# Layer 0's input product in two halves of its contraction, in a two-layer attention encoder

## The chip, the cores and the metric

The kernel runs on one core of one Trainium2 chip. The metric is device time of one execution in microseconds (us), and less is better. The engines are TensorE (PE in the profile; its weight loads are PEld), VectorE (DVE), ScalarE (ACT), GpSimd (POOL) and SyncE (SP), whose queue issues nearly all DMA transfers, in program order.

## The reference

One sequence of 256 tokens, width 2048, passes two layers. Each layer makes six modulation vectors from a conditioning vector, projects the normed and modulated stream by one wide matrix, runs two kinds of attention on the pieces, joins them in an output projection, and adds an MLP. The inputs and all weights are float32.

```python
cond = jax.nn.silu(c)
for l in range(DEPTH):
    mod = cond @ w_ada[l] + b_ada[l]                  # 2048 -> 6 * 2048
    sh_a, sc_a, g_a, sh_m, sc_m, g_m = split(mod, 6)
    h = _rmsnorm(x) * (1.0 + sc_a) + sh_a
    proj = h @ w_in[l]                                # 2048 -> 3904
    # dq 1024 | dk 1024 | dv 1024 | cq 512 | ckv 256 | kr 64
    out_a = _diff_attention(dq, dk, dv, positions, rel_bias_table, lam, subln_g, lambda_init)
    q  = _rmsnorm(cq, q_norm_g[l]) @ w_uq[l]          # 8 heads, 128 + 64 rotated
    kv = _rmsnorm(ckv, kv_norm_g[l]) @ w_ukv[l]       # 8 heads, 128 keys + 128 values
    out_b = _mla_attention(q_nope, q_rope, k_nope, k_rope, v_m)
    x = x + g_a * (concat([out_a, out_b]) @ w_o[l])
    h = _rmsnorm(x) * (1.0 + sc_m) + sh_m
    x = x + g_m * (square(relu(h @ w_mlp_in[l])) @ w_mlp_out[l])   # 2048 -> 8192 -> 2048
return _rmsnorm(x, final_norm_g)
```

The differential attention has 4 heads of two score maps each, with a bias that is looked up by bucketed distance between tokens. The multi-head latent attention (MLA below) has 8 heads with rotated parts.

## The kernel before

**Layout.** Features lie on the 128 partitions and tokens along the free axis, so x and h are 16 pieces of 128 x 256, one for each k (128 rows of the contraction). A tile of an output is 128 features by 256 tokens; two tiles share one of the eight PSUM banks (512 floats per partition).

**Two ways to multiply.** *Split*: `weights()` (L137) loads up to 1 MB into a buffer of the tag `raw`, ScalarE copies each half to a rounded `hi` (L146), VectorE subtracts to get `lo` (L147), and a tile takes three matmuls for each k (hi x hi, hi x lo, lo x hi; L182 to L184 in `mac()`, L253 to L255 for values, whose tokens lie on partitions). *Native*: the float32 weights are loaded straight into buffers of the tags `hi` and `lo` (L228) and multiplied without any split (L239); a matmul of this kind shows two records in the trace. Tags `hi` and `lo` have 4 buffers each, `raw` has 5.

**Modulation.** `ada_load()` (L289) brings one 128 x 2048 block (1 MB) of `w_ada` into a `raw` buffer, and `ada_sums()` (L297) multiplies it by the conditioning row `cond` on VectorE and sums along the row, which makes one column of one modulation vector. There are 192 such blocks in all. Every second sum is followed by a small operation that adds the constant part for two columns (L311 or L313). `ada_need()` brings all blocks up to one that is about to be used. Beside that each call of `weights()` adds a rate (`self.rate`) to a credit, and a block is loaded for each whole credit; the rate is `RATE_A0` = 1.1 in layer 0's attention. Layer 0's first 32 blocks, shift and scale, are needed by the input product.

**The head of layer 0.** `setup()` (L329) puts on the queue: the conditioning row, small tables, four modulation blocks, x, and ten more blocks (`LEAD`). The squares of x are summed by ScalarE and VectorE (`sumsq()`, L474 and L478) and finished by four matmuls with a constant matrix (L487), a root and a reciprocal (L489, L490). `norm_then_by_k()` (L587) then goes over eight steps p of two k each. A step brings the modulation that it needs, makes h for two k (`modulated()`: ht on VectorE L561, rounded and plain h on ScalarE, the low part on VectorE L563), and multiplies 12 tiles: cq, ckv and the first six tiles of dq. The first six steps (`WHOLE`) are native, the last two split. After each step comes a filler from a list: lambdas, the four parts of the position bias, the rotation tables. `EARLY` puts three of four loads of `w_d` (four more tiles: k heads 0 and q head 3) into the last steps.

**The rest of the attention.** `layer()` (L607) then has keys of the rotated part, six more columns of dk (`w_t`, one tile over all k in a call) with the score maps (`probs`) of the heads between them, the up-projections, and the values: eight loads of `w_dv`, split, in two groups of columns, interleaved with the steps of the MLA heads. Each MLA head has three steps: scores (psm) and softmax, transposes (pt), product with values (pom). The output projection (`w_oa`, `w_ob`) and the norm ahead of the MLP follow.

**What sets the order.** In all of this the order of each engine's instructions is decided by the framework's scheduler, not by the program text alone; in the MLP TensorE follows the text. The queue of SP issues loads in order, and a load whose buffer is still in use holds back all loads behind it.

Of the kernel before, what the change touches and what calls it, by code (L numbers as in the profile page):

```python
# [10 lines left out]
F32 = mybir.dt.float32  # L11
# [82 lines left out]
EARLY = {5: (0,), 6: (1, 2)}  # L94
LEAD = 10
WHOLE = 6
# [4 lines left out]
RATE_A0, RATE_A1, RATE_A2, RATE_K, RATE_M = 1.1, 0.5, 0.7, 0.6, 0.66  # L101
FILL = "lb|0|1|2|3|r"


class Trunk:
# [170 lines left out]
    def ada_plan(self):  # L276
        self.mod, self.macc = {}, {}
        for l in range(DEPTH):
            for g in range(6):
                self.mod[l, g] = self.cp.tile([P, NK], F32, name=f"mod{l}{g}")  # L280
                self.macc[l, g] = (self.cp if l else self.fp).tile([P, NK], F32, name=f"macc{l}{g}")
        for l in range(DEPTH):
            for gs in ((0, 1), (2,), (3, 4), (5,)):
                self.ada_todo += [(l, g, 2 * q + i) for q in range(8) for g in gs for i in range(2)]

# [6 lines left out]
    def ada_sums(self, after=None):  # L292

        nc = self.nc
        for w, l, g, i in self.ada_here:
# [10 lines left out]
            if i % 2:  # L306
                c = slice(i - 1, i + 1)
                v = V_BADA + 96 * l + NK * g + i
                b = self.vec[:, v - 1 : v + 1]
# [19 lines left out]
    def setup(self):  # L329
# [4 lines left out]
        nc.sync.dma_start(row, io["c"])  # L334
        self.mean = {}
        for n in (D, 2 * P):
            self.mean[n] = cp.tile([P, P], F32, name=f"mean{n}")
            nc.gpsimd.memset(self.mean[n], 1.0 / n)
        for j in range(4):
# [4 lines left out]
        self.vec = cp.tile([P, NVEC], F32, name="vec")  # L344
        nc.sync.dma_start(self.vec, io["vec"])
        self.eps = cp.tile([P, 1], F32, name="eps")
        nc.gpsimd.memset(self.eps, EPS)
        self.K = cp.tile([P, NCONST], F32, name="K")
        nc.sync.dma_start(self.K, io["consts"])
        self.pos = cp.tile([P, T + 8], I32, name="pos")  # L350
        nc.sync.dma_start(self.pos, io["pos"])
        self.ident = cp.tile([P, P], F32, name="ident")
        make_identity(nc, self.ident)
        self.x = cp.tile([P, NK, T], F32, name="x")
        self.ada(4)
        for q in range(4):
            nc.sync.dma_start(self.x[:, 4 * q : 4 * q + 4], io["xT"][:, 4 * q : 4 * q + 4])
        acc = None
        for k in range(0, NK, 2):
            acc = self.sumsq(acc, self.x[:, k : k + 2])  # L360
        self.ada(LEAD)
        return acc

    def fills(self):
        m = {"l": self.lambdas, "r": self.rope_setup, "b": self.bias_setup}
        m.update({str(a): lambda a=a: self.bias_part(a) for a in range(4)})
        return [(lambda w=w: [m[c]() for c in w]) for w in FILL.split("|")]

# [42 lines left out]
    def bias_part(self, a):  # L411
# [12 lines left out]
        ps = self.bank("pb")  # L424
        out = ps.rearrange("p a b -> p (a b)")
        for g in range(8):
# [3 lines left out]
            nc.vector.tensor_scalar(oh, sq.rearrange("p a b -> p (a b)"), K[:, C_W2 + g : C_W2 + g + 1], None, ALU.is_le)  # L430
            c = slice((g % 4) * P, (g % 4) * P + P)
            nc.tensor.matmul(out, lh[g // 4][:, c], oh, start=g == 0, stop=False)
            nc.tensor.matmul(out, ll[g // 4][:, c], oh, start=False, stop=g == 7)
        for h in range(HD):
            nc.scalar.activation(self.bias[32 * a : 32 * a + 32, h], ps[32 * h : 32 * h + 32], AF.Copy, scale=-1.0)

# [44 lines left out]
    def rstd(self, acc, n):  # L481
# [3 lines left out]
        acc = acc[:2] + acc[3:]  # L485
# [121 lines left out]
    def layer(self, l, acc, st):  # L607
# [3 lines left out]
        later = []  # L611

        def next_by_k(kqs):
            def f(h):
                if not later:
                    later.extend(self.open_banks(2))
                for kq in kqs:
                    self.by_k(later, [io["w_d"][l, kq]], h, 4 * kq, NK)
            return f

        if l == 0:
            early = {p: next_by_k(kqs) for p, kqs in EARLY.items()}
            h, banks = self.norm_then_by_k(l, acc, 0, 1, io["w_a"], 3, WHOLE, self.fills(), early)
            done = sum(len(k) for k in EARLY.values())
# [22 lines left out]
        def col(i, out, scale):  # L647
            def f():
                if i % 2 == 0:
                    self.ps = self.bank("ps")  # L650
                self.tile_cols(self.ps[:, i % 2], io["w_t"][l, i], h)
                if i % 2:
                    out.append(self.copy(self.ps, "k", scale))
            return f

# [17 lines left out]
        def val(cg, kq):  # L673
            def f():
                if kq == 0:
# [3 lines left out]
                self.tokens_by_k(self.pv, w, h[4 * kq : 4 * kq + 4], kq == 0, kq == 3)  # L679
                if kq == 3:  # L680
                    v.append([self.copy(ps, "v").rearrange("p a b -> p (a b)") for ps in self.pv])
            return f
# [16 lines left out]
        if l == 0:  # L699
            next_by_k(range(done, 4))(h)  # L700
            q += [self.copy(ps, "q", qs) for ps in banks[3:]]
            ckv += self.latent([ckr], gkv)
            kk.append(self.copy(later[0], "k", -1.0))
            q.append(self.copy(later[1], "q", qs))
            keys()
            order = [(0, kk, -1.0), (2, kk, -1.0), (4, kk, -1.0)]
            for n, (i, dst, scale) in enumerate(order):
                col(i, dst, scale)()
                if n == 0:
                    cq += self.latent(cqr, gq)  # L710
                probs(n)()
# [425 lines left out]
```

## Time and profile before

| | |
|---|---|
| time, median of 3 executions | 2238.68 us (2237.43 to 2238.83) |
| the profiled execution | 2236.12 us, of which its span is 2234.3 |
| TensorE busy | 2157.3 us, 97% of the span, 12254 matmul records |
| VectorE busy | 1618.6 us, 72% |
| ScalarE busy | 1151.2 us, 52% |
| moved by DMA | 585.40 MB, mean 262 GB/s |
| modulation blocks | 192 of 1024 KB, 4.9 us each from issue to landing |

The shares are means over the whole program: the two MLPs and layer 1 are most of it, and what the change touches lies in the first 444 us. A row of the groups gives the line, the engine, the operation, out<-in with shapes, the count, then the busy time in us and the mean in ns, then the idle time of the engine just ahead of these instructions with what ended it. A row of the timeline begins with the start and the length in us and ends, in brackets, with the wait ahead of it. A row of the waits view has the total in us, the number of waits and the longest.

### The profile page before, as it was taken

Reading aid. Unit: us, or ns where it says so; the run is one execution under the profiler, and the core shown is the slowest. Engines: PE = TensorE matmul, PEld = TensorE weight load, DVE = VectorE, ACT = ScalarE, POOL = GpSimd, SP = SyncE. Lnnn points to the kernel's source line nnn. Section 1 sums busy time; section 2 is a strip of 40 time slices with the busy share of each in tenths; the row PEclk is TensorE's granted clock in tenths of the full one; section 3 lists DMA queues with packets and bytes.
Section 4 is the critical chain, followed back from the end, with each engine's and each line's share of the span. In section 5 each row is a group of like instructions: output and inputs, shape, how many; then the busy total and the mean of one; then the engine's idle time right before and its main releaser. Section 6 shows DMA issues by size and latency. Waiting matters only on the chain.

```text
span 2234.3 us, 30873 instructions
## 1 busy us (share of the span) xinstructions
PE 2157.3 (97%) x12254; PEld 1899.1 (85%) x12254; DVE 1618.6 (72%) x2141; ACT 1151.2 (52%) x1705; POOL 25.3 (1%) x43
## 2 busy tenths in 40 slices
PE   2999999899999999999999999999999999999997
PEld 1899889898888888888888898999888888888886
DVE  7889778988778778777899876788545545544555
ACT  2655655346455355446455555647545535534643
POOL 0000000000000000000001000001000000000000
PEclk9999999999999999999999999999999999999999
DMA  9988677878888878888877765675554555555551
GB/s 370 342 328 302 246 282 301 334 282 334 331 306 322 315 303 322 330 309 320 320 269 282 262 257 215 239 288 201 198 198 175 202 190 191 191 200 189 188 189 57
DMA packets 84677, 585.40 MB, mean 262 GB/s; under 512 B 9394, under 2 KB 9778, under 8 KB 18482
## 3 DMA queue, kind: packets, MB, share of 16 engines
q1 hardware_dynamic: 84530, 583.42, 70.4%
q8 instruction: 96, 1.57, 0.3%
q14 instruction: 51, 0.41, 0.0%
HBM read 581.28 MB, written 2.10 MB: 261 GB/s over the span
## 4 chain that ended last, share of the span: by engine, by line
PE 91%; DVE 5%; DMA 1%; issue 1%; ACT 1%; SPq 0%; DVEq 0%; ACTq 0%
PE ps L203 21%; PE ps L206 11%; PE py L843 10%; PE py L841 10%; PE py L845 10%; PE pk L183 2%; PE ps L183 2%; PE ps L182 2%; PE ps L184 2%; PE pk L184 2%; PE pk L182 2%; PE pk L239 2%; DVE ada L297 2%; PE pv L253 1%; PE pv L254 1%; PE pv L255 1%
## 5 line engine op out<-in xcount | busy, mean ns | idle before, releaser
L147 DVE TENSOR_TENSOR lo<-raw,hi 128x1024 fp32r<-128x1024 f32 (+1 forms) x720 | 851.3, 1195 | 486.4 <-ACT hi L146 331.0
L146 ACT ACTIVATE hi<-raw 128x1024 fp32r<-128x1024 f32 (+1 forms) x720 | 742.6, 1036 | 690.7 <-PE py L845 370.2
L203 PE MATMUL ps<-h,hi 128*128 128x512 f32 x2016 | 472.9, 391 | 0.0
L297 DVE SCALAR_TENSOR_TENSOR ada<-ada,cond 128x2048 f32<-128x2048 f32 x192 | 437.9, 2284 | 6.9 <-ACT cond L343 6.9
L203 PEld LDWEIGHTS ps<-h,hi 128*128 128x128 f32 x2016 | 375.0, 188 | 75.8 <-DVE h L563 0.2
L841 PE MATMUL py<-hi,hid 128*128 128x512 f32 x1024 | 326.0, 389 | 0.0
L843 PE MATMUL py<-lo,hid 128*128 128x512 f32 x1024 | 326.0, 389 | 0.0
L845 PE MATMUL py<-hi,hid 128*128 128x512 f32 x1024 | 325.7, 389 | 0.0
L206 PEld LDWEIGHTS ps<-h,lo 128*128 128x128 f32 x2016 | 250.5, 192 | 5.0
L206 PE MATMUL ps<-h,lo 128*128 128x256 f32 x2016 | 252.0, 283 | 0.0
L843 PEld LDWEIGHTS py<-lo,hid 128*128 128x128 f32 x1024 | 192.2, 188 | 40.5 <-DVE lo L147 0.7
L845 PEld LDWEIGHTS py<-hi,hid 128*128 128x128 f32 x1024 | 192.2, 188 | 40.0
L841 PEld LDWEIGHTS py<-hi,hid 128*128 128x128 f32 x1024 | 191.7, 188 | 39.1
L879 ACT ACTIVATE sum<-ps 128x256 f32<-128x256 f32 x110 | 42.1, 383 | 116.4 <-PE ps L206 115.9
L182 PE MATMUL pk<-h,hi 128*128 128x256 f32 x304 | 86.6, 288 | 6.3 <-ACT h L562 6.3
L183 PE MATMUL pk<-h,hi 128*128 128x256 f32 x304 | 87.0, 287 | 0.9 <-DVE h L563 0.7
L184 PE MATMUL pk<-h,lo 128*128 128x256 f32 x304 | 86.8, 286 | 0.0
L239 PE MATMUL pk<-hf,w 128*128 128x256 f32 x288 | 65.2, 388 | 21.2 <-DMA w<-in_w_a 21.2
L176 DVE TENSOR_TENSOR hid<-relu,hid 128x256 fp32r<-128x256 f32 x128 | 48.3, 420 | 47.4 <-ACT hid L175 47.4
L239 PEld LDWEIGHTS pk<-hf,w 128*128 128x128 f32 x288 | 55.9, 195 | 29.9 <-issue 21.9
L182 PEld LDWEIGHTS pk<-h,hi 128*128 128x128 f32 x304 | 58.9, 195 | 6.9 <-ACT h L562 6.9
L183 PEld LDWEIGHTS pk<-h,hi 128*128 128x128 f32 x304 | 59.4, 195 | 1.3 <-DVE h L563 1.3
(226 smaller groups left out, 2792.6 us busy)
## 6 DMA issues: line engine op xcount, KB each, us to landing
raw<-in_w_m SPq DMA_DIRECT2D x238, 1024.0 KB, 4.8
ada<-in_w_ada SPq DMA_DIRECT2D x192, 1024.0 KB, 4.9
raw<-in_w_ob SPq DMA_DIRECT2D x24, 1024.0 KB, 4.9
raw<-in_w_dv SPq DMA_DIRECT2D x16, 1024.0 KB, 4.8
raw<-in_w_q SPq DMA_DIRECT2D x16, 1024.0 KB, 4.8
raw<-in_w_n SPq DMA_DIRECT2D x16, 768.0 KB, 6.0
w<-in_w_a SPq DMA_DIRECT2D x24, 384.0 KB, 6.0
raw<-in_w_a SPq DMA_DIRECT2D x12, 768.0 KB, 5.2
```

The source lines that it names most:

```text
L146: nc.scalar.activation(hi, v, AF.Copy)
L147: ins = nc.vector.tensor_tensor(lo, v, hi.bitcast(F32), ALU.subtract)
L182: mm(ps, hi, x[0], start=first, stop=False, skip_group_check=shared)
L183: mm(ps, hi, x[1], start=False, stop=False, skip_group_check=shared)
L184: mm(ps, lo, x[0], start=False, stop=last, skip_group_check=shared)
L203: mm(ps.rearrange("p a b -> p (a b)"), part(w, 0, k), both, start=k == 0, stop=False)
L206: mm(ps[:, 0], part(w, 1, k), x, start=False, stop=k == nk - 1)
L239: self.nc.tensor.matmul(ps, w[i][:, j * P : j * P + P], whole[i], start=first, stop=last, skip_group_check=True)
L297: ins = nc.vector.scalar_tensor_tensor(w, w, 1.0, self.cond, ALU.mult, ALU.mult, accum_out=acc[:, i : i + 1])
L841: mm(o, xh[:, tok], hi[:, part[j]], start=start, stop=False)
L843: mm(o, xh[:, tok], lo[:, part[j]], start=False, stop=False)
L845: mm(o, xl[:, tok], hi[:, part[j]], start=False, stop=stop)
```

## The change

The input product of layer 0 is cut anew, both in its columns and along its contraction.

- `setup()` puts x ahead of all modulation blocks on the queue, and issues none of them itself. The bias tables and the rotation tables are made right at the start.
- The squares of x are no longer added on VectorE: 16 tiles of squares go through 16 float32 matmuls with the constant matrix (`plain`).
- A new function `head()`, in which TensorE follows the program text, has two loops. The first goes over k = 0 to 7 (`NSPLIT`), native: two modulation blocks, 384 KB of `w_f1` and 512 KB of `w_v1`, h of one k, six tiles of late columns (last of dq and dk) and the values dv of all 1024 columns as four matmuls of 512 columns. Into it go bias parts 0 and 1: their marks (the one-hot rows made from distances by squares on ScalarE and a comparison on VectorE) at k = 2 and 4 and their products at k = 4 and 7.
- The seven banks of these partial results are copied out (`part_f`, `part_v`). The second loop multiplies 16 tiles (cq, ckv, dq heads 0 to 2, dk heads 0 and 1) split, over all 16 k, with 1 MB of `w_b` for each k and a rate of 1.25 modulation blocks for each of these loads.
- Behind it stand bias parts 2 and 3, the lambdas, then `rest_feats()`: the late columns over k = 8 to 15, split, joined to `part_f` on VectorE. The values over k = 8 to 15 are four split loads instead of eight, two of them among the score maps and two among the MLA steps, joined to `part_v` on VectorE.
- `RATE_A0` goes from 1.1 to 1.4. The first 32 modulation blocks come k by k, shift and scale in turn, and each gets its own small operation for one column.

```diff
-EARLY = {5: (0,), 6: (1, 2)}
-LEAD = 10
-WHOLE = 6
+NSPLIT = 8
+MARKS = {2: 0, 4: 1}
+PRODUCTS = {4: 0, 7: 1}
-RATE_A0, RATE_A1, RATE_A2, RATE_K, RATE_M = 1.1, 0.5, 0.7, 0.6, 0.66
-FILL = "lb|0|1|2|3|r"
+RATE_H, RATE_A0, RATE_A1, RATE_A2, RATE_K, RATE_M = 1.25, 1.4, 0.5, 0.7, 0.6, 0.66
+    def head(self):
+        self.setup()
+        self.bias_setup()
...
+            nc.scalar.activation(t, self.x[:, k : k + 2], AF.Square)
...
+        r = self.rstd(sq, D, True)
+        self.rope_setup()
...
+        for k in range(NSPLIT):
+            for _ in range(2):
+                self.ada_load()
+            w = []
+            for name, tag, n in (("w_f1", "hi", 768), ("w_v1", "lo", 1024)):
+                w.append(self.wp.tile([P, n], F32, tag=tag, name=self.name("w"), bufs=4))
+                nc.sync.dma_start(w[-1], io[name][0, k])
+            self.ada_sums()
...
+            t = normed(k)
+            nc.scalar.activation(fs[k], t, AF.Identity, bias=sh[:, k : k + 1])
+            for j in range(6):
+                ps = feats[j // 2][:, j % 2]
+                mm(ps, w[0][:, j * P : j * P + P], fs[k], start=k == 0 and j % 2 == 0,
+                   stop=k == NSPLIT - 1 and j % 2 == 1, skip_group_check=True)
+            for t in range(2):
+                for cg in range(2):
+                    mm(flat(vals[cg][t]), fs[k][:, t * P : (t + 1) * P], w[1][:, cg * 512 : cg * 512 + 512],
+                       start=k == 0, stop=k == NSPLIT - 1)
+            if k in MARKS:
+                marks[MARKS[k]] = self.bias_marks(MARKS[k])
+            if k in PRODUCTS:
+                self.bias_products(PRODUCTS[k], marks.pop(PRODUCTS[k]))
+        ready(0)
+        ready(1)
+        self.part_f = [self.copy(ps, "pf", s) for ps, s in zip(feats, (-1.0, qs, -1.0))]
+        self.part_v = [[flat(self.copy(ps, "pvp")) for ps in y] for y in vals]
+        self.rate = RATE_H
+        banks = self.open_banks(8)
+        for k in range(NK):
+            for i, w in enumerate(self.weights(io["w_b"][0, k])):
+                for j in range(8):
+                    b = 4 * i + j // 2
+                    self.mac(banks[b][:, j % 2], w, j * P, P, h[k], k == 0 and j % 2 == 0, k == NK - 1 and j % 2 == 1, True)
+            if k + 2 < NK:
+                ready(k + 2)
+        return h, banks
+    def rest_feats(self, h):
...
+            for i, w in enumerate(self.weights(self.io["w_f2"][0, p], 1536)):
...
+        for ps, t, s in zip(banks, self.part_f, (-1.0, qs, -1.0)):
+            self.nc.vector.scalar_tensor_tensor(t, ps, s, t, ALU.mult, ALU.add)
...
+                elif kq == 3:
+                    for ps, part in zip(self.pv, self.part_v[cg]):
+                        nc.vector.tensor_tensor(part, ps.rearrange("p a b -> p (a b)"), part, ALU.add)
...
             ckv += self.latent([ckr], gkv)
...
+            self.bias_part(2)
+            self.bias_part(3)
+            self.lambdas()
+            k2, q3, k3 = self.rest_feats(h)
+            cq += self.latent(cqr, gq)
...
+            probs(0)()
             keys()
...
+            probs(1)()
+            for kq in (2, 3):
+                val(0, kq)()
+            probs(2)()
...
-            [val(cg, kq) for cg in range(2) for kq in range(4)],
+            [val(cg, kq) for cg in range(2) for kq in range(4)] if l else [val(1, kq) for kq in (2, 3)],
```

How this moves instructions, at four places. First VectorE at the start, from the reciprocal of the norm (rstd) to the first normed piece (ht). Before:

```order
L297 SCALAR_TENSOR_TENSOR ada_177,macc_80<-ada_177,cond 128x2048
L490 RECIPROCAL rstd_215<-rstd_215 128x256
L297 SCALAR_TENSOR_TENSOR ada_180,macc_80<-ada_180,cond 128x2048
L297 SCALAR_TENSOR_TENSOR ada_184,macc_82<-ada_184,cond 128x2048
L313 TENSOR_TENSOR mod_79<-macc_80,vec 128x2
L561 SCALAR_TENSOR_TENSOR ht_224<-x,mod_81,rstd_215 128x256 x2
```

The same place after the change, where rr and cc are steps of the rotation tables:

```order
L583 RECIPROCAL rstd_196<-rstd_196 128x256
L540 SCALAR_TENSOR_TENSOR rr_201<-kk_200,rr_201 128x256
L312 SCALAR_TENSOR_TENSOR mod_83<-macc_84,vec 128x1
L540 SCALAR_TENSOR_TENSOR rr_201<-kk_200,rr_201 128x256 x4
L297 SCALAR_TENSOR_TENSOR ada_256,macc_82<-ada_256,cond 128x2048
L543 TENSOR_SCALAR rr_201<-rr_201 128x256
L314 TENSOR_TENSOR mod_81<-macc_82,vec 128x1
L547 TENSOR_SCALAR cc_216<-rr_201 128x256
L381 SCALAR_TENSOR_TENSOR ht_243<-x,mod_83,rstd_196 128x256
```

One modulation sum instead of two stands between them, and seven steps of the rotation tables that stood later.

Second, ScalarE where the first loop passes into the second; pf and pvp are the copies of the native banks pk and pv, and hi the rounded first weights of the second loop:

```order
L409 ACTIVATE hf_496<-ht_522,mod_81 128x256
L271 ACTIVATE pf_562<-pk_223 128x512
L271 ACTIVATE pf_564<-pk_224 128x512
L145 ACTIVATE hi_586<-raw_584 128x1024
L271 ACTIVATE pf_566<-pk_225 128x512
L271 ACTIVATE pvp_568<-pv_226 128x512
L145 ACTIVATE hi_590<-raw_584 128x1024
```

The first rounded weights come behind two copies of banks that the last native step must have finished.

Third, TensorE at the end of the head, behind the split tiles; before, the latent's norm (pn) and the keys (pkr):

```order
L487 MATMUL pn_1303<-acc_1301,mean_108 128x256 x2
L182 MATMUL pkr_1320<-h_225,hi_1323 128x256
L183 MATMUL pkr_1320<-h_225,hi_1323 128x256
L184 MATMUL pkr_1320<-h_225,lo_1324 128x256
```

After the change, where pb is the bias product of the marks oh, and pk the late columns:

```order
L580 MATMUL pn_1664<-acc_1662,mean_121 128x256 x2
L521 MATMUL pb_1717<-oh_1687,lsch_152 128x512
L522 MATMUL pb_1717<-oh_1687,lscl_153 128x512
...
L521 MATMUL pb_1717<-oh_1715,lsch_158 128x512
L522 MATMUL pb_1717<-oh_1715,lscl_159 128x512
L521 MATMUL pb_1778<-oh_1748,lsch_152 128x512
L522 MATMUL pb_1778<-oh_1748,lscl_153 128x512
L456 MATMUL pl_1801<-vec,mean_119 128x4
L181 MATMUL pk_1810<-h_1038,hi_1815 128x256
```

All 16 products of bias part 2 now stand ahead of the first matmul of the late columns. Their first mark stands on VectorE behind these rows (lo_1816 to lo_1871 are the late columns' weights, ckr the latent):

```order
L297 SCALAR_TENSOR_TENSOR ada_1531,macc_86<-ada_1531,cond 128x2048
...
L146 TENSOR_TENSOR lo_1816<-raw_1813,hi_1815 128x768
L146 TENSOR_TENSOR lo_1820<-raw_1813,hi_1819 128x768
L297 SCALAR_TENSOR_TENSOR ada_1593,macc_86<-ada_1593,cond 128x2048
L583 RECIPROCAL rstd_1667<-rstd_1667 128x256
L297 SCALAR_TENSOR_TENSOR ada_1595,macc_86<-ada_1595,cond 128x2048
...
L146 TENSOR_TENSOR lo_1871<-raw_1864,hi_1870 128x768
L504 TENSOR_SCALAR rel_1677<-rel_1677 128x512
L297 SCALAR_TENSOR_TENSOR ada_1826,macc_86<-ada_1826,cond 128x2048
L510 TENSOR_SCALAR oh_1687<-sq_1685,K 128x512
```

Four modulation sums and four halves of the late columns' weights come ahead of the mark that the products wait for.

Fourth, TensorE among the last MLA steps. Before, with values (pv) between the steps:

```order
L253 MATMUL pv_2608<-hi_2776,h_898 128x512
L961 MATMUL pt_2764<-ident,sm_2696 128x128
L1026 MATMUL pom_2771<-aT_2716,vm_2218 128x256
L961 MATMUL pt_2764<-ident,sm_2696 128x128 x3
L1026 MATMUL pom_2771<-aT_2716,vm_2220 128x256
L254 MATMUL pv_2608<-lo_2777,h_898 128x512
L255 MATMUL pv_2608<-hi_2776,h_898 128x512
```

After the change:

```order
L1091 MATMUL psm_2952<-kn_2364,qn_2724 128x256
L1092 MATMUL psm_2952<-kr_2142,qr_2539 128x256
L1043 MATMUL pt_2968<-ident,sm_2886 128x128 x4
L1108 MATMUL pom_2949<-aT_2947,vm_2623 128x256
L1108 MATMUL pom_2949<-aT_2947,vm_2625 128x256
L1091 MATMUL psm_2952<-kn_2364,qn_2724 128x256
L1092 MATMUL psm_2952<-kr_2142,qr_2539 128x256
```

The last MLA steps follow one another with no value product between them.

164 lines of the change are left out of this document (93 added, 71 removed).

## The prediction

> **What bounds the kernel now.** The page's first line comes first, then the windows view, cut where the stages change hands; its columns are each engine's busy time with its instructions, the granted TensorE clock, the DMA share and the rate.
>
> ```profile
> span 2234.3 us, 30873 instructions
> ```
>
> ```profile
> core 0: us, PE busy (x) PEld busy (x) DVE busy (x) ACT busy (x) POOL busy (x), PEclk, DMA share, GB/s
> 0.00:48.40 48.40, 9.24 (x12) 3.66 (x12) 35.75 (x49) 12.36 (x20) 1.02 (x9) 1.00 0.94 376
> 48.40:127.20 78.80, 78.76 (x353) 68.25 (x354) 71.56 (x130) 43.99 (x76) 0.53 (x1) 1.00 0.83 313
> 127.20:170.50 43.30, 41.99 (x341) 41.26 (x341) 37.14 (x45) 21.86 (x29) 0.00 (x0) 1.00 0.94 365
> 170.50:249.80 79.30, 70.88 (x528) 67.57 (x527) 72.31 (x129) 42.90 (x76) 0.00 (x0) 0.98 0.80 299
> 249.80:334.10 84.30, 83.91 (x418) 70.22 (x416) 61.67 (x97) 49.37 (x95) 0.00 (x0) 1.00 0.70 262
> 334.10:443.60 109.50, 101.29 (x815) 99.12 (x813) 93.46 (x116) 49.21 (x79) 0.00 (x0) 0.98 0.84 317
> 443.60:2234.30 1790.70, 1771.21 (x9796) 1549.02 (x9796) 1246.65 (x1581) 931.52 (x1332) 23.80 (x33) 0.99 0.68 249
> 140.00:150.00 10.00, 10.00 (x85) 10.00 (x85) 10.00 (x11) 2.50 (x3) 0.00 (x0) 1.00 0.97 378
> 200.00:210.00 10.00, 7.78 (x47) 7.29 (x47) 8.55 (x19) 3.12 (x6) 0.00 (x0) 0.83 0.95 383
> ```
>
> The rows are: the start; the native stage; the split end of the head; keys, columns and up-projections; attention with the values; the output projection and its norm; and from 443.6, the first matmul of layer 0's MLP, everything else. There TensorE works 1771.2 of 1790.7 us, and the change edits nothing in it. So the new time is the old one moved by what happens to 443.6. Ahead of that TensorE works 386.1 us and stands 57.5, of which 39.2 in the first row; VectorE works 371.9 and stands 71.7 (12.7, 7.2, 6.2, 7.0, 22.6, 16.0 by row). The two are close: a start earlier for TensorE pays only so far as VectorE follows. VectorE also holds the weights: this is the queue's own row of the waits view.
>
> ```profile
> SPq L158 <- DVE lo L147: 770.7, 199, 9.3
> ```
>
> A weight load waits for a buffer that VectorE has not read out yet, 199 times in the program. A late VectorE thus makes late weights.
>
> **Part 1, the earlier start.** From the timeline, engine by engine (start, length, instruction, wait ahead of it):
>
> ```profile
> 2.67 7.16 PE L342 MATMUL pc<-c_row,mean 1*128 1x512 f32 x8 [2.67 <-DMA c_row<-in_c]
> 25.13 2.08 PE L487 MATMUL pn<-acc,mean 128*128 128x256 f32 x4 [15.30 <-DVE acc L478]
> 48.44 12.57 PE L239 MATMUL pk<-hf,w 128*128 128x256 f32 x48 [21.23 <-DMA w<-in_w_a]
> ```
> ```profile
> 9.86 31.86 SPq L289 DMA_DIRECT2D ada<-in_w_ada  x10
> 41.77 14.41 SPq L228 DMA_DIRECT2D w<-in_w_a  x10
> ```
> ```profile
> 16.79 4.41 ACT L477 ACTIVATE sqx<-x 128x512 f32<-128x512 f32 x7
> 27.29 1.28 ACT L489 ACT_TABLE_LOAD   x1 [6.09 <-PE pn L487]
> 28.59 0.47 ACT L489 ACTIVATE rstd<-pn,eps 128x256 f32<-128x256 f32 x1
> ```
>
> Now ten modulation loads hold the queue until 41.8, and the first native matmul runs at 48.4. Behind the change only two stand ahead of the first weights, and x ahead of both, so the bound is the chain to h. The conditioning row's products end at 9.8 and its last activation, of 0.6, about 10.5; the squares follow, the first by 11.1. In place of seven VectorE additions and four matmuls, 32 mean matmuls on TensorE trail the squares: the first eight at the 0.52 of the four cold ones above, the others at 0.22 (Part 2), 9.4 us, to 20.5. Table load and root (1.9) and the reciprocal (1.8, its row in Part 4) give 24.2. Then VectorE's new order has five rope steps (0.43 each), one whole modulation sum (2.4) and small ones (0.9) ahead of the first ht: it starts at 29.6, ends at 30.1, its bias on ScalarE at 30.6, and the first matmul runs at **30.6, 17.8 earlier**.
>
> **Part 2, the native stage.** A native step of 24 tile-steps has 48 records in 10.5 (the 12.57 above is the first and cold one, 2.05 longer). That is 0.438 for one tile and one k. The new stage has 14 x 8 = 112 of them, 49.0 us, with 2.05 for the cold start; two bias parts of 16 products at 0.23 add 7.3; and one wait, where the hf of k = 5 stands behind four bias copies on ScalarE:
>
> ```profile
> 83.18 2.37 ACT L435 ACTIVATE bias<-pb 32x512 f32<-32x512 f32 x4
> ```
>
> 2.4 + 0.5 = 2.9. 30.6 + 49.0 + 2.1 + 7.3 + 2.9 = 91.9. A k-step brings 2.9 MB, 7.7 us at the first row's 376 GB/s, close to the 6.1 of its matmuls; loads run ahead through four buffers of each kind, and I take no wait for them.
>
> The rule to weigh here: the first native step was cold (12.57), and the window at 200, with 2.2 us idle, had a granted clock of 0.83. The Trainium skill ("TensorE: Matmul & The Clock Gate", sections "The HAM clock gate" and "HAM oscillation — how this bites in real kernels") says that an idle window of about 3.4 us halves the clock and that work paced by transfers can go cold at every k. The trace agrees with the first half at 48.4, and shows no native step but the first cold. By the rule the 2.9 wait costs nothing more, and the sum stays.
>
> **Part 3, VectorE's account to the MLP.**
>
> ```profile
> L297 DVE SCALAR_TENSOR_TENSOR ada<-ada,cond 128x2048 f32<-128x2048 f32 x73 | 166.1, 2283 | 6.9 <-ACT cond L343 6.9
> L147 DVE TENSOR_TENSOR lo<-raw,hi 128x1024 fp32r<-128x1024 f32 x80 | 97.1, 1221 | 32.2 <-ACT hi L146 31.7
> L430 DVE TENSOR_SCALAR oh<-sq,K 128x512 fp32r<-128x512 f32 x32 | 14.4, 484 | 6.4 <-ACT sq L428 5.1
> L147 DVE TENSOR_TENSOR lo<-raw,hi 128x768 fp32r<-128x768 f32 x12 | 11.2, 954 | 0.8 <-ACT hi L146 0.8
> L478 DVE TENSOR_TENSOR acc<-acc,sqx 128x512 f32<-128x512 f32 x14 | 9.6, 688 | 0.7
> L561 DVE SCALAR_TENSOR_TENSOR ht<-x,mod,rstd 128x256 f32<-128x256 f32 x19 | 8.5, 480 | 0.1
> ...
> L313 DVE TENSOR_TENSOR mod<-macc,vec 128x2 f32<-128x2 f32 x22 | 3.4, 152 | 0.1
> ```
>
> Native tile-steps fall from 144 to 112, so 2 MB more are split: four more lo of 1024 (84 for 80; the 768 wide stay 12): 4 x 1.22 = **+4.9**. Seven additions go: 7 x 0.69 = **-4.8**. The two halves of seven bank results are joined, three for the late columns and four for the values, none of which the trace has: nothing if they only fill VectorE's idle time, 0.69 each by the additions of the same shape, which I take: **+4.8**. Sixteen more single-column modulations at 0.15: **+2.4**. By the new order 78 sums instead of 73 stand ahead of the MLP's first matmul (the rates of 1.25 and 1.4): 5 x (2.28 + 0.08 for its read) = **+11.8**; fewer are left for the rest, where TensorE is the bound and they bring nothing. Together +19.1: 371.9 becomes **391.0**. TensorE loses 32 x (0.438 - 3 x 0.118) = 2.7, the split price being 85 records in 10 us, and gains 28 mean matmuls in idle time.
>
> **Part 4, what VectorE waits for.** By stage:
> - Start: 14 (12.7 before), since c, x and the squares must come in all the same.
> - Native stage: 3.5, beside that wait of TensorE.
> - The seam, **10**: the first split weights' hi are queued on ScalarE among the copies of the native banks, and the lo on VectorE need them. VectorE runs out of ready work about 10 us ahead of the native end. At nothing, if its modulation sums last; at 13, if none is there.
> - Sixteen split steps, 5.65 of TensorE (48 x 0.118) and on VectorE 2.44 + 1.25 x 2.37 + ht, h: 6.0 or more where h is made. Loads and sums share five buffers; I take half a us a step, **8** (3 to 16).
> - Head's end, **8**. Here TensorE's fixed order has bias part 2 ahead of the late columns. VectorE has, between the last lo of the loop and the first mark, four sums (9.5), four 768 lo (3.8), the reciprocal, two lt, latl and the marks' differences, by these rows:
>
> ```profile
> L420 DVE SCALAR_TENSOR_TENSOR rel<-fl,rt 128x256 f32<-128x256 f32 x8 | 3.8, 481 | 0.1
> L419 DVE TENSOR_SCALAR rt<-fh 128x256 f32<-128x256 f32 x8 | 2.8, 348 | 0.0
> L448 DVE SCALAR_TENSOR_TENSOR rr<-kk,rr 128x256 f32<-128x256 f32 x6 | 2.6, 425 | 0.2
> L490 DVE RECIPROCAL rstd<-rstd 128x256 f32<-128x256 f32 x1 | 1.8, 1753 | 1.8 <-ACT rstd L489 1.8
> L423 DVE TENSOR_SCALAR rel<-rel 128x512 f32<-128x512 f32 x4 | 1.7, 426 | 0.1
> ```
>
> 1.8 + 1.0 + 0.7 + 0.7 + 1.0 + 0.4 + 0.3 for mods = 5.9, so 19.2 in all, less the 2.8 for which TensorE still works: TensorE stands about **15** us with the late columns' weights lying ready behind it. VectorE works all that time; it waits afterwards, as weight buffers held by those matmuls and the squares on ScalarE come late. Nothing at best, 14 at worst.
> - Joining 2.5, attention 6 (its 22.6 of before go, because the values' first half has left TensorE there), output projection to MLP 10 (16.0 before; four more sums).
>
> 14 + 3.5 + 10 + 8 + 8 + 2.5 + 6 + 10 = 62. 391.0 + 62 = **453.0, 9.4 later than 443.6**. The break-even is an idle time of 52.6. TensorE agrees: its 386.1 + 3.4 leave 63.5 idle: about 15 at the start, 3 in the native stage, 10 in the split steps, 15 and then some 12 more around the bias products, 8 in the output projection's norm as before, none elsewhere.
>
> Against the profiled execution's own 2236.1 (span 2234.3 and 1.8 around it) this is 2245.5. The median of the runs shown, 2238.7, lies 2.6 above that execution: **2248.1**.
>
> **The rivals.**
> *A, the early start carries.* If the head's end costs VectorE nothing, the seam 5 and the loop 4, its idle time is 62 - 8 - 5 - 4 = 45 and the MLP starts at 436.0: **2231.1, faster**. It decides at 52.6. For it: the start's 48.4 us fall by about 18 in every reading, and with native steps running VectorE was idle in only 7.2 of 78.8 us before. Against it: every modulation sum moved forward must run before 443.6 as before, and TensorE's wait for bias part 2 is written into its order.
> *C, the attention's tail lengthens.* Two value products stand between the MLA steps where eight stood. A step's own chain is:
>
> ```profile
> L930 ACT ACTIVATE sm<-sm,mxm 128x256 f32<-128x256 f32 x16 | 8.0, 502 | 4.9 <-DVE sm L1011 4.7
> L1014 ACT ACTIVATE sm<-sm,r 128x256 f32<-128x256 f32 x16 | 7.2, 500 | 5.6 <-DVE r L933 5.6
> L272 ACT ACTIVATE aT<-pt 128x512 f32<-128x512 f32 x12 | 7.1, 589 | 1.7 <-PE pt L961 1.6
> L1011 DVE TENSOR_SCALAR_CACHE_REDUCE sm<-psm 128x256 f32<-128x256 f32 x16 | 6.7, 420 | 3.2 <-PE psm L1010 3.2
> ```
>
> Two of each of the first, second and fourth and one copy: 3.4 a head. Uncovered in five heads that is 17, at most: half of it on top of the forecast gives **2256.6**. Against it: VectorE's modulation sums fill this time in the forecast already.
> *D, a cold native stage.* If TensorE goes cold at each k, seven more steps of 6.1 take twice that, 43 longer: **2291**. No native step after the first was cold. The skill's page named above has it as its rule on transfers.
> *E, it does nothing.* What is won at the start is lost in the later waits exactly, as VectorE's total decides: **2238.7**.
>
> **How the numbers follow.** Forecast 0.52, A 0.26, C 0.13, D 0.02, E 0.07. A measurement of this kernel can tell about 0.2% (4.5 us) from no change. The forecast's own range is 2238 to 2262, and 0.16 of its 0.52 falls within 4.5 us; 0.02 of A and all of E do too. Same: 0.25; faster: 0.24; slower: 0.36 + 0.13 + 0.02 = 0.51. The range leaves out A's best tenth (idle below 40) and most of C and D: **2226 to 2264**.
>
> **What would show it.** Right: the first native matmul near 30; a stop of about 15 us of TensorE ahead of the bias products near 190 to 205; VectorE's busy time to the MLP's first matmul near 391; that matmul near 453. Wrong: VectorE's idle time to there below 52 (A), a hole at each MLA step (C), native steps of 12 us (D), or a native stage that waits for its weights.

## The result: slower, by four times what was forecast

| | before | after |
|---|---|---|
| median | 2238.05 us (4 runs, 2236.26 to 2238.83) | 2275.36 us (4 runs, 2270.57 to 2278.85) |
| ratio after to before | | 1.0166, 95% interval 1.0147 to 1.0186 |
| span of the profiled execution | 2234.3 | 2277.1 |
| first native matmul | 48.4 | 30.1 (forecast 30.6) |
| native stage ends | 127.2 | 93.2 (91.9) |
| output projection starts | 334.1 | 358.4 |
| MLP's first matmul | 443.6 | 484.3 (453.0) |
| VectorE busy to there | 371.9 | 388.6 (391.0) |
| VectorE idle to there | 71.7 | 95.7 (62) |

The forecast was 2248.1, range 2226.0 to 2264.0: the sign was right and the size was not. The profiled execution after is the longest of its four (2278.85), so its 42.8 us on the span is 5.5 more than the medians' 37.3.

The windows view of the kernel after, cut at its own stages: start, native stage, split loop, head's end with the late columns, score maps and up-projections, the last MLA steps, output projection with its norm, and the rest.

```profile
core 0: us, PE busy (x) PEld busy (x) DVE busy (x) ACT busy (x) POOL busy (x), PEclk, DMA share, GB/s
0.00:30.10 30.10, 16.34 (x41) 9.91 (x41) 17.54 (x37) 14.12 (x21) 1.02 (x9) 0.92 0.93 363
30.10:93.20 63.10, 60.22 (x192) 39.59 (x193) 49.45 (x84) 25.21 (x47) 0.00 (x0) 0.93 0.84 342
93.20:189.70 96.50, 93.61 (x769) 92.39 (x768) 83.42 (x99) 40.46 (x52) 0.00 (x0) 1.00 0.94 356
189.70:242.40 52.70, 33.22 (x187) 28.50 (x188) 37.36 (x59) 28.86 (x42) 0.53 (x1) 0.74 0.46 166
242.40:298.80 56.40, 48.98 (x285) 41.78 (x284) 55.08 (x112) 28.93 (x58) 0.00 (x0) 0.94 0.75 285
298.80:358.40 59.60, 54.10 (x271) 44.69 (x269) 43.19 (x81) 37.69 (x81) 0.00 (x0) 0.94 0.67 251
358.40:484.30 125.90, 106.85 (x814) 102.56 (x812) 102.52 (x125) 49.09 (x79) 0.00 (x0) 0.95 0.81 301
484.30:2277.10 1792.80, 1771.95 (x9796) 1550.97 (x9796) 1235.57 (x1568) 932.71 (x1332) 21.34 (x33) 0.99 0.67 246
```

40.7 of the 42.8 us lie ahead of the MLP, as the forecast had it. Up to 189.7 nothing is lost against the forecast: in the split loop VectorE stands 5 us longer than forecast, but TensorE is busy for 93.6 of the loop's 96.5 us. Then come three stages in which neither engine is full: 189.7:242.4 (TensorE 33.2 of 52.7, VectorE 37.4), 298.8:358.4 (VectorE 43.2 of 59.6) and 358.4:484.3 (TensorE 106.9 of 125.9, VectorE 102.5), the last against 109.5 us for the same stage before.

The wait ahead of the bias products, from TensorE's timeline of the kernel after; the row ahead of it is the latent's norm:

```profile
189.72 1.10 PE L580 MATMUL pn<-acc,mean 128*128 128x256 f32 x4 [1.25 <-issue]
205.85 0.77 PE L521 MATMUL pb<-oh,lsch 128*128 128x512 f32 x1 [15.03 <-DVE oh L510]
```

15.0 us, as forecast. And the queue of SP around the start of the output projection at 358.4 (start, length, what is issued):

```profile
333.09 0.33 SPq L157 DMA_DIRECT2D raw<-in_w_oa  x1
345.56 0.33 SPq L289 DMA_DIRECT2D ada<-in_w_ada  x1
347.77 0.33 SPq L157 DMA_DIRECT2D raw<-in_w_oa  x1
367.76 2.93 SPq L289 DMA_DIRECT2D ada<-in_w_ada  x2
373.42 0.33 SPq L157 DMA_DIRECT2D raw<-in_w_ob  x1
```

In 40 us it issues three weight loads and three modulation blocks. For 31.3 of them it stood, ahead of two blocks, until VectorE had made the low parts that free a buffer, as its waits view from 333 to 374 shows:

```profile
SPq L289 <- DVE lo L146: 31.3, 2, 19.6
```

VectorE meanwhile works half of the time, by this row of the windows view:

```profile
330.00:360.00 30.00, 26.69 (x122) 21.45 (x121) 14.83 (x36) 17.32 (x43) 0.00 (x0) 0.89 0.43 167
```

Right behind, the output projection asks for 12 MB of weights with 1.4 blocks for each call.

### The profile page after: what moved, and what is told of

It reads as the page before. It is cut to its first block, busy times and chain, and to the rows that moved or that the text cites. A ratio compares the mean times of both kernels' runs of the same rounds, so it can differ in the third digit from the quotient of the medians.

```text
span 2277.1 us, 31049 instructions
## 1 busy us (share of the span) xinstructions
PE 2185.3 (96%) x12346; PEld 1910.4 (84%) x12346; DVE 1624.1 (71%) x2161; ACT 1157.1 (51%) x1707; POOL 22.9 (1%) x43
## 4 chain that ended last, share of the span: by engine, by line
PE 85%; DVE 9%; DMA 3%; ACT 2%; issue 1%; DVEq 0%; ACTq 0%
PE ps L202 20%; PE ps L205 11%; PE py L923 10%; PE py L925 10%; PE py L927 10%; DVE ada L297 3%; DVE lo L146 2%; PE pk L181 2%; PE pk L183 2%; PE pk L182 2%; PE ps L183 1%; PE ps L182 1%; PE ps L181 1%; DMA raw<-in_w_b 1%; PE pv L416 1%
## 5 line engine op out<-in xcount | busy, mean ns | idle before, releaser
L181 PE MATMUL pk<-h,hi 128*128 128x256 f32 x496 | 141.7, 286 | 5.8 <-ACT h L655 5.8
L183 PE MATMUL pk<-h,lo 128*128 128x256 f32 x496 | 142.0, 286 | 1.7 <-DVE lo L146 1.5
L182 PE MATMUL pk<-h,hi 128*128 128x256 f32 x496 | 141.7, 286 | 0.0
L181 PEld LDWEIGHTS pk<-h,hi 128*128 128x128 f32 x496 | 96.3, 195 | 6.6 <-ACT h L655 6.2
L183 PEld LDWEIGHTS pk<-h,lo 128*128 128x128 f32 x496 | 96.6, 195 | 2.8 <-DVE lo L146 2.5
L182 PEld LDWEIGHTS pk<-h,hi 128*128 128x128 f32 x496 | 96.5, 195 | 0.2
L181 PE MATMUL ps<-moh,hi 128*128 128x256 f32 x192 | 55.9, 291 | 6.7 <-ACT hi L145 6.7
```

The lines of the kernel that those rows point to most:

```text
L181: mm(ps, hi, x[0], start=first, stop=False, skip_group_check=shared)
L182: mm(ps, hi, x[1], start=False, stop=False, skip_group_check=shared)
L183: mm(ps, lo, x[0], start=False, stop=last, skip_group_check=shared)
```

## The experiments

Each is compared with the kernel before on the same chip, whose medians lay between 2237.2 and 2237.8, or in microseconds with the 2275.36 after the change. "The MLP" below is its first matmul in the profiled execution, "scores" the first MLA score matmul.

**1. The rate back to 1.1.**

```diff
-RATE_H, RATE_A0 = 1.25, 1.4
+RATE_H, RATE_A0 = 1.25, 1.1
```

> RATE_A0 back from 1.4 to 1.1, all else as after the change. Theory R (rate): from the output projection on, a weight load brings VectorE 2.44 + 1.4 x 2.37 = 5.8 us and a pair of tiles 13.2 us with its updates, against 11.3 us of TensorE, so VectorE became the pace of that stage. Then the stage from the output projection's first matmul to the MLP's first falls from 125.9 to about 111 us and the whole time by 12 to 20 us. Rival B (buffers): the stage is long because loads were held back in the attention's tail; then it stays above 120 and the time moves by less than 5 us.

2267.72 us (2 runs), 7.6 less than after the change. From the output projection to the MLP:

```profile
362.00:470.40 108.40, 101.29 (x814) 99.09 (x812) 87.14 (x108) 48.44 (x79) 0.00 (x0) 0.99 0.77 284
```

The stage is 108.4 instead of 125.9, below the 111 of theory R, and TensorE takes 101.3 instead of 106.9, at a granted clock of 0.99 instead of 0.95. Rival B, which kept the stage above 120, falls. So the rate did set the pace there. Whether by VectorE's work or by the transfers this run does not tell, since each sum takes its block's transfer with it. The whole time missed the 12 to 20 us of theory R: the projection begins 3.6 later, and behind the MLP's first matmul 4.8 us are added, where 69 sums instead of 78 have been done: half of the gain is given back.

**2. The bias behind the late columns.**

```diff
-            self.bias_part(2)
-            self.bias_part(3)
-            self.lambdas()
             k2, q3, k3 = self.rest_feats(h)
+            self.bias_part(2)
+            self.bias_part(3)
+            self.lambdas()
```

> Bias parts 2 and 3 and the lambdas behind the late columns instead of ahead of them. Theory Q (order): TensorE's 15.0 us wait for the first mark goes, the late columns start near 195 instead of 219, and the whole time falls by 8 to 15 us. Rival V (VectorE's total decides): the wait turns up again at the score maps, which need the bias, and the time falls by less than 4 us.

2274.18 us, 1.2 less: nothing that can be told from no change. The late columns' last matmul came at 214.9 instead of 241.4, and the scores came at 299.5 instead of 298.8, so 26 us were won and lost again within 85. VectorE from 190 to 300:

```profile
190.00:300.00 110.00, 82.87 (x473) 69.50 (x474) 97.36 (x175) 59.59 (x102) 0.53 (x1) 0.89 0.67 250
```

97.4 of 110 us. A hole in TensorE's row was removed where VectorE was the bound. Rival V held here.

**3. Four value loads among the MLA steps.**

```diff
-            for kq in (2, 3):
-                val(0, kq)()
-            [val(cg, kq) for cg in range(2) for kq in range(4)] if l else [val(1, kq) for kq in (2, 3)],
+            [val(cg, kq) for cg in range(2) for kq in range(4)] if l else [val(cg, kq) for cg in range(2) for kq in (2, 3)],
```

> The first column group's two value loads move from the score maps to the MLA steps, so four instead of two stand there. Theory F (filler): the stage from the first MLA scores to the output projection, where VectorE stood 16.4 us and TensorE 5.5 us, loses its holes and the whole time falls by 5 to 10 us. Rival: the score maps, which lose their filler, give it back, and the time moves by less than 3 us either way.

2283.44 us, 8.1 more. The stage of the MLA steps grew from 59.6 to 64.1 with 7.5 us more of TensorE in it, and the score maps ahead of it did not become shorter (scores at 299.1). Both the theory and its rival missed; filler for TensorE was not what lacked.

**4. The earlier start alone, on the kernel before.**

```diff
-LEAD = 10
+LEAD = 4
-        self.ada(4)
         for q in range(4):
             nc.sync.dma_start(self.x[:, 4 * q : 4 * q + 4], io["xT"][:, 4 * q : 4 * q + 4])
+        self.ada(4)
```

> The kernel before with x ahead of all modulation blocks and LEAD 4 instead of 10: the earlier start alone, without the cut in halves. Theory V (what VectorE and the queue must bring sets the end of the native stage): the first native matmul moves from 48.4 to about 30 to 36 us, native steps stretch beyond 10.5 us as each now brings 7 MB, and the MLP's first matmul moves by 0 to 5 us. Rival: the start carries, and the time falls by 10 us or more.

2235.53 us (8 runs), ratio 0.9994, interval 0.9983 to 1.0006. The first native matmul came at 31.5 instead of 48.4, 16.9 earlier, and the MLP at 442.7 instead of 443.6. The 63 us behind the start:

```profile
31.50:94.50 63.00, 56.92 (x242) 48.04 (x242) 58.82 (x102) 27.43 (x48) 0.00 (x0) 0.97 0.94 376
```

TensorE now waits in the native stage, with VectorE at 58.8 of 63 and the transfers at 0.94. On this kernel an early start by itself is worth about one of its 16.9 us.

**5. The blocks where VectorE stands.** Nearly the same number of sums, in other places:

```diff
+        light = mla[6:] + [av[0][0], av[1][0]]
+        if l == 0:
+            self.rate = 0.8
+            light = [g for i, f in enumerate(light) for g in ([f, lambda: self.ada(1)] if i % 2 else [f])]
         self.interleave(
             [val(cg, kq) for cg in range(2) for kq in range(4)] if l else [val(1, kq) for kq in (2, 3)],
-            mla[6:] + [av[0][0], av[1][0]],
+            light,
         )
```

> As after the change, but the modulation blocks come where VectorE stands: nine extra blocks among the last MLA steps, and a rate of 0.8 instead of 1.4 from there to the MLP. Theory P (place): VectorE's 16.4 us of idle time in the stage of the last MLA steps and the overfull output projection are one fault, since blocks are loaded only with weights and that stage has few; then the tail stays within 3 us of 59.6, the output projection falls from 125.9 to about 108, and the time falls by 14 to 20 us. Rival V (VectorE's total alone decides): the number of sums ahead of the MLP hardly changes, so the time moves by less than 5 us.

2261.14 us, 14.2 less (the code sets ten extra blocks, not nine). The last MLA steps and the output projection:

```profile
298.30:364.60 66.30, 57.21 (x270) 46.79 (x269) 61.47 (x102) 37.58 (x81) 0.00 (x0) 0.90 0.88 337
364.60:469.40 104.80, 101.12 (x815) 99.11 (x813) 81.86 (x102) 50.37 (x79) 0.00 (x0) 1.00 0.78 287
```

VectorE's work moved from the second (102.5 to 81.9) to the first (43.2 to 61.5). The second lost 21.1 us, the first gained 6.7, more than the 3 that theory P allowed. 77 sums instead of 78 stand ahead of the MLP, so it is not their number. Rival V falls here.

**6. All bias parts in the native stage.**

```diff
-MARKS = {2: 0, 4: 1}
-PRODUCTS = {4: 0, 7: 1}
+MARKS = {0: 0, 2: 1, 4: 2, 5: 3}
+PRODUCTS = {2: 0, 4: 1, 6: 2, 7: 3}
-            self.bias_part(2)
-            self.bias_part(3)
```

> All four bias parts in the native stage (marks at k = 0, 2, 4, 5, products at 2, 4, 6, 7) instead of two there and two at the head's end. Theory Q: the 15.0 us wait and the cold products at the head's end go, VectorE uses the 10 us in which it stood at the seam, the native stage ends 8 to 14 us later, the first MLA scores come 8 to 15 us earlier, and the time falls by 8 to 15 us. Rival V: VectorE does the same work in the same time, and the time falls by less than 4 us.

2262.99 us, 12.4 less; the two runs (2259.03 and 2266.96) lie 8 us apart, so this size is rough. The split loop ends 7.0 later (196.8 for 189.7), the late columns' last matmul comes at 222.8 instead of 241.4, the scores at 284.7 instead of 298.8. The 63 us behind the first native matmul (the native stage now ends at 101.7), and from there to the scores:

```profile
31.80:94.80 63.00, 59.14 (x201) 39.84 (x202) 54.56 (x100) 32.29 (x55) 0.00 (x0) 0.96 0.82 319
94.80:284.70 189.90, 172.48 (x1230) 161.37 (x1230) 168.32 (x249) 90.36 (x140) 0.53 (x1) 0.96 0.83 316
```

In those 63 us VectorE works 54.6 instead of 49.5: it makes part of the marks in time that it had idle, and what stood behind them goes faster. Beside experiment 2 this says: the marks had to leave the stretch where VectorE is full, and moving them within it was worth nothing.

**7 and 8. A warm TensorE at the bias products.**

```diff
-            self.bias_part(2)
+            marks = self.bias_marks(2)
+            with self.tc.manual_schedule(engines={mybir.EngineType.PE}):
+                idle = self.bank("pd")
+                for i in range(24):
+                    nc.tensor.matmul(idle[:, 0], self.mean[D], self.x[:, i % 2], start=i == 0, stop=i == 23)
+                self.bias_products(2, marks)
```

> As after the change, with 24 float32 matmuls that nobody reads put into TensorE's 15 us wait ahead of bias part 2, so that its products run warm. Theory C (cold clock): the 16 products fall from about 0.43 to 0.23 us each, the late columns end 3 to 6 us earlier and the time falls by as much. Rival V: VectorE and ScalarE pace the products, and the time moves by less than 2 us.

2271.34 us, 4.0 less, with runs (2269.90 to 2272.79) that overlap those after the change; the late columns' last matmul came at 241.8, as late as without. The added matmuls ran out 4.67 us ahead of the first product, which was as slow as ever, so this did not try the question, and the 4.0 us are not the gain of a warm clock. With 34 of them:

> As warm, with 34 unread matmuls in place of 24, so that they reach to the first bias product (in warm a gap of 4.67 us was left, and the products still began at 0.79 us each). Theory C (cold clock): the 16 products of part 2 now run at about 0.23 to 0.25 where their marks are there, the late columns end 3 to 6 us earlier, and the first MLA scores come as much earlier. Rival V: VectorE and ScalarE pace what follows; the products may be shorter, but the first MLA scores stay within 2 us of 298.8.

2273.69 us. First rows with a wait, from TensorE's timeline of that run:

```profile
190.91 14.84 PE L786 MATMUL pd<-x,mean 128*128 128x256 f32 x68
206.10 0.47 PE L521 MATMUL pb<-oh,lsch 128*128 128x512 f32 x1 [0.35 <-DVE oh L510]
207.45 0.50 PE L521 MATMUL pb<-oh,lsch 128*128 128x512 f32 x1 [0.64 <-DVE oh L510]
208.82 0.50 PE L521 MATMUL pb<-oh,lsch 128*128 128x512 f32 x1 [0.64 <-DVE oh L510]
```

The first products of a pair now take 0.47 and 0.50 instead of 0.77 to 0.80, and the third pair waits 0.64 for its mark, where it had no wait after the change. The scores come at 298.2 instead of 298.8. So the cold clock of these first products cost nothing, since their marks paced them. Only the first six ran warm; the next are slow again, as the last section shows. No run kept TensorE warm from the score maps to the MLP, so what the cold clock cost there stays open.

**9. Both gains together (5 and 6).**

> The edits of spread and biasnat together. If each removes its own wait, their gains add up to 22 to 35 us, and the kernel comes within 1% of the one before. If VectorE's total decides, together they give less than 8 us.

2246.19 us (5 runs), 29.2 less than after, ratio to before 1.0033 (1.0017 to 1.0049). Apart they gave 14.2 + 12.4 = 26.6: they add up.

**10. Fewer blocks in the split loop, alone.**

```diff
-RATE_H = 1.25
+RATE_H = 1.0
```

> As after the change, with RATE_H 1.0 instead of 1.25, so four blocks fewer in the split loop. If VectorE paces the loop (96.5 us against 90.4 of matmuls), the loop falls by 3 to 6 us; the blocks come back later, and the whole time moves by less than 4 us.

2273.7 us, 1.7 less. The loop did not get shorter: it ended at 193.2, 3.5 later. With four blocks fewer the later k's modulation is no longer ahead of its use: ScalarE waits 35.5 us of the loop for normed pieces (ht), after the change 11.4. The sums that the rate adds were not what paced the loop.

**11 and 12. Fewer blocks up to the scores, on top of 9.** First with both rates and the last one:

```diff
-RATE_H, RATE_A0 = 1.25, 1.4
+RATE_H, RATE_A0 = 1.1, 0.8
-            self.rate = 0.8
+            self.rate = 1.0
```

> spreadbias with fewer blocks where VectorE is full: RATE_H 1.1 instead of 1.25, RATE_A0 0.8 instead of 1.4 up to the last MLA steps, 1.0 from there. Theory P: in spreadbias VectorE worked 166.9 of the 189.8 us between the native stage and the first MLA scores, and the output projection left it 23 us; about ten sums move from the first to the second or later, the scores come 5 to 10 us earlier, and the time falls to 2236 to 2242 us. Rival W (waits, not work, fill those 190 us): under 2 us.

**2226.99 us** (4 runs, 2226.27 to 2229.36), ratio to before **0.9955, interval 0.9939 to 0.9972**: faster than both kernels, and 9 us below the range of theory P. From the native stage to the scores, the last MLA steps, the output projection:

```profile
94.80:267.10 172.30, 166.41 (x1238) 156.66 (x1237) 154.32 (x233) 93.20 (x145) 0.53 (x1) 1.00 0.83 310
267.10:330.20 63.10, 54.33 (x271) 45.72 (x269) 57.02 (x99) 35.62 (x81) 0.00 (x0) 0.95 0.83 321
330.20:434.90 104.70, 101.03 (x815) 99.06 (x813) 89.30 (x110) 50.29 (x79) 0.00 (x0) 0.99 0.83 315
```

In the first of these 12.6 us of VectorE's work left, against experiment 9, and the stage lost 17.5. Ahead of the MLP stand 72 sums instead of 77. Then the one rate alone:

> spreadbias with RATE_A0 0.8 instead of 1.4 up to the last MLA steps and nothing else changed (RATE_H stays 1.25, 0.8 behind). tuned, which also has RATE_H 1.1 and 1.0 behind, gained 19 us on spreadbias. Theory P: the stretch from the late columns to the first MLA scores was overfilled by this rate, so this edit alone gives 12 us or more of the 19. Rival: the split loop's rate was the cause, and this edit gives less than 6.

2240.51 us (8 runs, 2236.77 to 2243.83), 5.7 less than experiment 9, so just under the rival's bound by medians, while the scores came 10.4 us earlier in its profiled execution. The other two edits make the remaining 13.5. In the profiled executions the two kernels lie 10.5 us apart, and 7.1 of them come ahead of the first score, where the loop's rate is the only edit that tells them apart. So it seems to make the larger part here, though experiment 10 shows that by itself it gives little; the two were not tried apart.

**13. The same remedy on the kernel before.** Experiment 4 with five extra blocks among the MLA steps and a rate of 0.9 from there:

```diff
+        if l == 0:
+            self.rate = 0.9
+            light = [g for i, f in enumerate(light) for g in ([f, lambda: self.ada(1)] if i % 4 == 3 else [f])]
```

> The kernel before with x first and LEAD 4 (as in b_early), five extra blocks among the MLA steps, where VectorE stood 22.6 us, and a rate of 0.9 instead of 1.1 from there to the MLP. Theory P: the output projection falls from 109.5 to 105 to 107 us without a longer attention, and the time falls to 2229 to 2234 us. Rival: TensorE bound both stages already (83.9 of 84.3 us, 101.3 of 109.5), and the time stays within 2 us of b_early's 2235.5.

2230.35 us (10 runs), ratio 0.9971 (0.9962 to 0.998). The output projection takes 105.9 instead of 109.5, with attention as long as in experiment 4 (85.2). So of the 10.4 us by which experiment 11 beats the kernel before, some 7 are had without the cut in halves; against this kernel the cut, with its blocks well placed, is 3.4 us faster by medians, with intervals that overlap a little.

## Why the prediction was wrong

**Part 1 and Part 2 held.** The first native matmul came at 30.1 for 30.6, and the native stage ended at 93.2 for 91.9; only the first native step and the one behind the bias copies (below) ran cold, so rival D was not there. The wait of 2.9 came as worked out, with a cold step behind it that the sum did not have (below).

**Part 3 held.** VectorE's work to the MLP was 388.6 for 391.0, with 78 sums and 84 wide lo as counted.

**Part 4 failed**, in the terms for VectorE's idle time: 95.7 instead of 62. By stage:

| stage | forecast | measured |
|---|---|---|
| start, native stage and seam | 27.5 | 26.2 |
| split loop | 8 | 13.1 |
| head's end | 8 | 15.3 |
| joining and attention | 8.5 | 17.7 |
| output projection to MLP | 10 | 23.4 |

*The output projection (+13.4).* I charged the rate of 1.4 as work, five sums of 2.4, and left the stage's idle time below that of before. But a block hangs on each weight load: 2.4 + 1.4 x 2.4 = 5.8 us of VectorE for 5.7 of TensorE, with the updates of x on top. Experiment 1 takes the stage from 125.9 to 108.4 by the rate, experiment 5 to 104.8. So the density of the blocks is the cause. Whether VectorE's work or the transfers passed it on is not shown. The 2.4 MB of a load and its blocks take, by an estimate from the 376 GB/s of the first row before the change, 6.7 us, longer than either engine's work; the forecast has no term for them here. From the first load of `w_ob` to the MLP both were about equally full, and ScalarE waited for the weights (the second row is from the waits view of the whole stage):

```profile
374.00:484.30 110.30, 91.25 (x704) 87.91 (x702) 93.56 (x111) 37.44 (x50) 0.00 (x0) 0.95 0.88 326
ACT hi L145 <- DMA raw<-in_w_ob: 20.8, 9, 4.6
```

*The attention (+9.2).* The forecast let VectorE's sums fill the MLA steps, and turned rival C down for the same reason. They could not: blocks are loaded only with weights, that stage issues six weight loads where before the change it issued eleven, and its queue stood, as shown above. VectorE stood 16.4 of 59.6 us. Rival C's price, 8.5 us on this term, came near the 9.2, but its mechanism, TensorE without filler, was not it: experiment 3 gave TensorE filler and lost 8 us, experiment 5 gave VectorE its sums and won 14.

*The head's end (+7.3).* The wait was forecast as about 15 and came as 15.0, in part by luck: 19.2 less 2.8 is 16.4, and VectorE did one of the four sums, and then stood 4.6 us, before TensorE's wait began. The price to VectorE was sized by hand at 8 and was 15.3. By VectorE's timeline some 8 of it are waits among the marks, their squares and their products, and some 7 are for the late columns' rounded weights from ScalarE, the kind of wait that the forecast named. Experiment 6 shows what the placement costs, some 12 us of the whole time; experiment 2 that moving it within the same stretch returns nothing.

*The split loop (+5.1).* This was no loss. TensorE was busy for 93.6 of the 96.5 us and the transfers ran at 0.94, so VectorE stood because it was not the pace there. By the forecast's own account for TensorE, 90.4 of matmuls and 10 of waits, the loop even came out 4 us shorter.

The rule on the clock: TensorE took 413.3 us to the MLP where the forecast's sum has 389.5. The kernel of experiment 11, with the same matmuls and a granted clock of 1.00 from the native stage to the scores and 0.99 in the output projection, takes 398. So some 15 of the 23.8 go with cold stretches (granted clock 0.74 at the head's end, 0.94 to 0.95 from the score maps to the MLP); the rest is not explained. The Trainium skill ("TensorE: Matmul & The Clock Gate", section "The HAM clock gate") says that an idle window of about 3.4 us brings the slow state back. The rows agree for long waits: behind 15.03 us a product took 0.77, behind 4.67 still 0.77, behind 0.35 only 0.47. But the wait of 2.9 us in the native stage, which the forecast let cost nothing more by that rule, was enough too, as TensorE's timeline after the change shows beside the step that follows:

```profile
69.71 4.53 PE L412 MATMUL pk<-hf,w 128*128 128x256 f32 x12 [2.88 <-ACT hf L409]
...
77.51 2.75 PE L412 MATMUL pk<-hf,w 128*128 128x256 f32 x12
```

1.8 us more for the same twelve records, at a granted clock of 0.50 from 70 to 73 us. The measurement decides: here less than 3.4 us of waiting brought the slow clock back. In experiment 8 the cold clock of the first products had no price; in the output projection it came and went with the rate (106.9 us at 1.4, 101.3 at 1.1).

Of the rivals, A missed although the start did come earlier: experiment 4 shows, on the kernel before, that the earlier start alone carries 0.9 of 16.9 us to the MLP. What stays open: whether VectorE's work or the transfers paced the output projection, what the cold clock cost from the score maps on, and whether the loop's rate made the larger part of the last step to experiment 11, as its trace suggests.

## What to carry to other kernels

A background job that is tied to another event (here one modulation block for each weight load) follows that event's density: when a change moves the events, look where the background work goes, stage by stage, and compare the time that one event takes on each engine and in the transfers. Here 16.7 us more of VectorE's work came with 40.7 us, in large part because of where they landed: experiment 9 takes 29.2 us back with 77 of the 78 sums still ahead of the MLP. And removing a wait of an engine that was not the bound of its stretch was worth nothing here until the work that it waited for left the stretch.

## What was not expected of the hardware

In experiment 8 TensorE, warm after 14.8 us of matmuls, went back to slow products at about 209.6, though no wait since then was longer than 0.64 us: its matmuls had filled 2.2 of the 3.5 us since the first product. The granted clock is 1.00 up to 209.5 and 0.50 from 210 to 213. From its timeline:

```profile
209.15 0.40 PE L522 MATMUL pb<-oh,lscl 128*128 128x512 f32 x1
209.60 0.55 PE L521 MATMUL pb<-oh,lsch 128*128 128x512 f32 x1
209.95 0.63 PE L522 MATMUL pb<-oh,lscl 128*128 128x512 f32 x1
210.37 0.63 PE L521 MATMUL pb<-oh,lsch 128*128 128x512 f32 x1
```

So a stretch with many short waits lost the fast clock here as one long wait does.
